# Row normalization on one core: the first store goes to ScalarE's queue, and VectorE alone does the last scale of its tile

## The chip, the cores and the metric

The kernel runs on one core of a Trainium2 chip. The metric is device time in microseconds (us), the median of several executions. A run counts as slow when it is over 1.5% above the fastest run of the same kernel; all runs quoted are fast unless the text says otherwise. A queue, here, is the line of transfers that one engine (SP or ScalarE) has issued; the 16 DMA engines carry out the transfers of all queues, one packet after another. A ratio is the mean time of one kernel's fast runs over the mean of the other's fast runs in the same rounds, so it is not quite the ratio of the medians quoted beside it.

## The reference

Each row of a 1024 x 4096 float32 matrix is divided by its length:

```python
norm = np.sqrt(np.sum(x ** 2, axis=-1, keepdims=True) + eps)
return (x / norm).astype(np.float32)
```

So 16.78 MB are read and 16.78 MB are written.

## The kernel before

There are two tiles ("tile 0" and "tile 1"), each with four rows per partition: 128 x (4 x 4096) float32, 8.39 MB. Both loads are issued at once on the queue of the SP engine. For each tile VectorE squares row 3 and ScalarE squares rows 0, 1 and 2, each with a running sum; ScalarE takes the roots, VectorE the reciprocals, and VectorE scales the rows in place. Only the last row to be ready in tile 0, row 2, is scaled by both engines:

```python
def scale_by_both(self, r):
    cut = 7 * self.D // 8
    rstd = self.rstd[:, r : r + 1]
    self.nc.scalar.activation(out=self.x[:, r, :cut], in_=self.x[:, r, :cut],
                              func=ACT_F.Copy, scale=rstd)
    self.nc.vector.tensor_scalar_mul(out=self.x[:, r, cut:],
                                     in0=self.x[:, r, cut:], scalar1=rstd)
...
for i in range(n_tiles):
    g = RowGroups(nc, io, stats, scratch, D, R, eps_t)
    load = nc.sync.dma_start(out=g.flat(), in_=x_t[i])
    ...
for i, g in enumerate(groups):
    ...
    g.square_act(2)
    g.norm(2)
    if i < n_tiles - 1:
        g.scale_by_both(2)
    else:
        g.scale(2)
    store = nc.sync.dma_start(out=out_t[i], in_=g.flat())
```

Four transfers of 8.39 MB stand in one queue: load 0, load 1, store 0, store 1. Each is spread over 16 DMA engines, and each engine moves 8 packets of 64 KiB per transfer, then one tiny packet that writes the semaphore.

## Time and profile before

| | before |
|---|---|
| time, median | 81.8 us (81.79 to 81.83) |
| span of the profiled execution | 80.2 us |
| DMA engines in packets, mean of 16 | 97.4% of the span, 78.1 us |
| VectorE / ScalarE busy | 33% / 37% |
| store 0 issued / load 1 seen landed | 38.99 / 41.40 us |

The queue line of the page says how long packets were under way, as a share of 16 engines' span. Multiplied by the span it is the packet time per engine.

### The profile page before, as it was taken

The page shows a single profiled execution, that of the slowest core. Times are in us where ns is not written, and L with a number is a line of the kernel's source. Part 1 is how long each engine was busy: PE and PEld are TensorE (multiplying, and loading weights), DVE is VectorE, ACT ScalarE, POOL GpSimd, SP SyncE. Part 2 cuts the span into 40 slices and gives each one's busy share as a digit, 9 for nine tenths or more (in the row PEclk, how much of TensorE's full clock was granted, in tenths as well). Part 3 has the DMA queues.
Part 4 walks back from the last instruction along what each step waited for, and adds up shares of the span by engine and source line. Part 5 has one row for each costly group of instructions (what it writes and reads, how often), then busy time and mean ns, then how long its engine had stood idle before and what let it go on. Part 6 is the DMA issues. An engine that isn't in the chain of part 4 may idle for free.

```text
span 80.2 us, 93 instructions
## 1 busy us (share of the span) xinstructions
DVE 26.7 (33%) x21; ACT 29.7 (37%) x23; POOL 0.2 (0%) x4
## 2 busy tenths in 40 slices
DVE  0000000000099599960039995999200000000000
ACT  6000000000099999989439999950000000000000
POOL 0000000000000000000000000000000000000000
DMA  9099996699996699996699990999991999992990
GB/s 490 33 523 523 523 490 294 261 523 523 523 490 261 294 523 523 523 490 261 294 523 523 523 490 33 523 523 523 523 458 65 523 523 523 523 425 98 523 523 0
DMA packets 576, 33.55 MB, mean 418 GB/s; under 512 B 64, under 2 KB 64, under 8 KB 64
## 3 DMA queue, kind: packets, MB, share of 16 engines
q1 hardware_dynamic: 576, 33.55, 97.4%
HBM read 16.78 MB, written 16.78 MB: 418 GB/s over the span
## 4 chain that ended last, share of the span: by engine, by line
DMA 51%; ACT 10%; DVE 9%; issue 0%
DMA xt<-in_x_dram 51%; ACT sq_act L33 9%; DVE xt L64 9%; ACT rstd L53 1%; DVE rstd L59 0%
## 5 line engine op out<-in xcount | busy, mean ns | idle before, releaser
L33 ACT ACTIVATE sq_act<-xt 128x4096 f32<-128x4096 f32 x6 | 21.7, 3609 | 22.4 <-DMA xt<-in_x_dram 22.4
L42 DVE SCALAR_TENSOR_TENSOR sq_dve<-xt 128x4096 f32<-128x4096 f32 x2 | 8.9, 4426 | 26.4 <-DMA xt<-in_x_dram 26.4
L64 DVE TENSOR_SCALAR xt<-xt,rstd 128x4096 f32<-128x4096 f32 x7 | 16.5, 2353 | 0.2
L72 ACT ACTIVATE xt<-xt,rstd 128x3584 f32<-128x3584 f32 x1 | 3.3, 3283 | 0.2 <-DVE rstd L59 0.2
L53 ACT ACTIVATE rstd<-ssq,eps_t 128x1 f32<-128x1 f32 x8 | 2.1, 290 | 0.1
L59 DVE RECIPROCAL rstd<-rstd 128x1 f32<-128x1 f32 x8 | 1.3, 160 | 2.5 <-ACT rstd L53 2.5
L33 ACT ACT_TABLE_LOAD x1 | 1.3, 1283 | 0.8 <-PEq L258 0.8
L53 ACT ACT_TABLE_LOAD x1 | 1.3, 1283 | 0.0
L33 ACT ACTIVATION_READ_ACCUMULATOR sq_act<-xt 128x1 f32 x6 | 1.1, 187 | 0.0
L78 DVE TENSOR_SCALAR xt<-xt,rstd 128x512 f32<-128x512 f32 x1 | 0.5, 487 | 0.0
L211 DVE MEMSET eps_t<- 128x1 f32 x1 | 0.1, 59 | 0.9 <-PEq L258 0.9
L42 DVE DVE_READ_ACCUMULATOR sq_dve<-xt 128x1 f32 x2 | 0.2, 83 | 0.0
L258 POOL MEMSET const-uint8-127<- 128x1 uint8 x1 | 0.1, 103 | 0.0
L258 POOL MEMSET const-bfloat16-1.0<- 128x1 bf16 x1 | 0.1, 102 | 0.0
L258 POOL MEMSET const-float32-0.0<- 128x1 f32 x1 | 0.1, 99 | 0.2 <-issue 0.2
L258 POOL MEMSET const-float32-1.0<- 128x1 f32 x1 | 0.1, 99 | 0.0
## 6 DMA issues: line engine op xcount, KB each, us to landing
xt<-in_x_dram SPq DMA_DIRECT2D x2, 31.3
out_dram<-xt SPq DMA_DIRECT2D x2, 22.5
```

The source lines that it names most:

```text
L33: self.nc.scalar.activation(out=sq_a, in_=self.x[:, r], func=ACT_F.Square, accum_out=self.ssq[:, r : r + 1],)
L42: self.nc.vector.scalar_tensor_tensor(out=sq_v, in0=self.x[:, r], scalar=1.0, in1=self.x[:, r], op0=ALU.mult, op1=ALU.mult, accum_out=self ...
L53: self.nc.scalar.activation(out=self.rstd[:, r : r + n], in_=self.ssq[:, r : r + n], func=ACT_F.Sqrt, bias=self.eps_t,)
L59: self.nc.vector.reciprocal(out=self.rstd[:, r : r + n], in_=self.rstd[:, r : r + n])
L64: self.nc.vector.tensor_scalar_mul(out=self.x[:, r], in0=self.x[:, r], scalar1=self.rstd[:, r : r + 1])
L72: self.nc.scalar.activation(out=self.x[:, r, :cut], in_=self.x[:, r, :cut], func=ACT_F.Copy, scale=rstd,)
L78: self.nc.vector.tensor_scalar_mul(out=self.x[:, r, cut:], in0=self.x[:, r, cut:], scalar1=rstd)
L211: nc.vector.memset(eps_t, eps)
L258: nc = _bacc.Bacc("TRN2", target_bir_lowering=False, num_devices=1)
```

## The change

The intent is to have tile 0 ready sooner (VectorE needs 2.35 us for the row; the shared scale needs 3.28 us on ScalarE) and to let its store go out without standing behind load 1 in SP's queue. The helper `scale_by_both` goes away, and:

```diff
-        if i < n_tiles - 1:
-            g.scale_by_both(2)
-        else:
-            g.scale(2)
-        store = nc.sync.dma_start(out=out_t[i], in_=g.flat())
+        g.scale(2)
+        queue = nc.scalar if i < n_tiles - 1 else nc.sync
+        store = queue.dma_start(out=out_t[i], in_=g.flat())
```

More of the change, by code (lines that the diff above doesn't have):

```diff
@@ L65, in scale @@
             out=self.x[:, r], in0=self.x[:, r], scalar1=self.rstd[:, r : r + 1]
-        )
-    def scale_by_both(self, r):
-        cut = 7 * self.D // 8
-        rstd = self.rstd[:, r : r + 1]
-        self.nc.scalar.activation(
-            out=self.x[:, r, :cut],
-            in_=self.x[:, r, :cut],
-            func=ACT_F.Copy,
-            scale=rstd,
-        )
-        self.nc.vector.tensor_scalar_mul(
-            out=self.x[:, r, cut:], in0=self.x[:, r, cut:], scalar1=rstd
         )
```

## The prediction

> **What bounds the kernel now.** I read the page's slices and its queue line first, because a kernel that loads and stores every byte once is likely to be held by its transfers.
>
> ```profile
> DMA  9099996699996699996699990999991999992990
> ...
> q1 hardware_dynamic: 576, 33.55, 97.4%
> ```
>
> One digit is 2.0 us. Digits drop to 6, 0 or 1 now and then, but a packet here is 64 KiB and long, and is booked unevenly; the second line is the safe one: on the mean of 16 engines the packets took 97.4% of the span, 0.974 x 80.2 = 78.1 us of 80.2. The 576 packets are 512 of 64 KiB (33.55 MB / 65,536) and 64 tiny ones, which are the semaphore writes: 16 for each of 4 transfers (2 loads, 2 stores, 8.39 MB each). So each engine moves 8 data packets per transfer, 32 in all, and one packet takes 78.1 / 32 = 2.44 us. Read one by one, the packet records say 2.418 us for nearly all of them, so a transfer lasts 8 x 2.418 = 19.3 us and four last 77.4 us.
>
> Then the groups of instructions, for the engines:
>
> ```profile
> DVE 26.7 (33%) x21; ACT 29.7 (37%) x23; POOL 0.2 (0%) x4
> ...
> L33 ACT ACTIVATE sq_act<-xt 128x4096 f32<-128x4096 f32 x6 | 21.7, 3609 | 22.4 <-DMA xt<-in_x_dram 22.4
> L42 DVE SCALAR_TENSOR_TENSOR sq_dve<-xt 128x4096 f32<-128x4096 f32 x2 | 8.9, 4426 | 26.4 <-DMA xt<-in_x_dram 26.4
> L64 DVE TENSOR_SCALAR xt<-xt,rstd 128x4096 f32<-128x4096 f32 x7 | 16.5, 2353 | 0.2
> L72 ACT ACTIVATE xt<-xt,rstd 128x3584 f32<-128x3584 f32 x1 | 3.3, 3283 | 0.2 <-DVE rstd L59 0.2
> ```
>
> Both engines are idle for two thirds of the time and wait for loads. Last the timeline around the first store:
>
> ```profile
> 35.68 3.28 ACT L72 ACTIVATE xt<-xt,rstd 128x3584 f32<-128x3584 f32 x1 [0.23 <-DVE rstd L59]
> ...
> 38.99 0.35 SPq L240 DMA_DIRECT2D out_dram<-xt  x1
> 41.40 3.62 ACT L33 ACTIVATE sq_act<-xt 128x4096 f32<-128x4096 f32 x1 [2.43 <-DMA xt<-in_x_dram]
> ...
> 54.38 2.35 DVE L64 TENSOR_SCALAR xt<-xt,rstd 128x4096 f32<-128x4096 f32 x1
> 56.76 0.34 SPq L240 DMA_DIRECT2D out_dram<-xt  x1
> ```
>
> The reader is to see three things. The first store is issued at 38.99, but load 1 has landed only at 41.37 (the squares start at 41.40), and both sit on the one SP queue, so the store is behind the load: it is 2.4 us early. In the packet records the load's last data packets end at 40.26 to 41.05 and the store's first start at 40.48 to 41.06: no hole worth having. The second store is issued at 56.76, while the first store's last packets end at 59.80 to 60.36: it has 3.0 to 3.6 us of slack. So the queue is never empty from about 1 to 79.7 us, and the end is set by 32 packets in a row on each engine. The chain of waits walks back through tile 1's arithmetic, but that is not what binds: the last store waits for the queue, not for its data.
>
> **What the Trainium skill says.** (1) "DMA: Bandwidth & Descriptors", section Specifications: a fabric ceiling of 435 GB/s. The trace agrees: 65,536 B x 16 / 2.418 us = 434 GB/s. There is no bandwidth left to win. (2) Same page, Issuing engines are not separate DMA queues: transfers from SP and ACT run on the same 16 engines and interleave; a second queue saves only issue time. The trace has only one queue, so it can't show this; it shows issues of 0.34 us, off the path. (3) Same page, Queues, rings and completion order: each DMA engine goes round-robin between its rings, one packet at a time, and the semaphore increment is a last small descriptor of the transfer's own ring. No run so far shows two rings, but the 64 tiny packets are these descriptors; this is where my main risk comes from. (4) "VectorE: DVE Perf Modes", The perf-mode tier table: a float32 tensor_scalar in SBUF runs at 2x (1227 ns for 2048 elements). The trace agrees: 2353 ns for 4096 is far under one element per 0.96 GHz cycle (4267 ns).
>
> **The change, part by part.** *Scale of tile 0, row 2.* Removed: ACT 3283 ns beside DVE 487 ns, both starting at 35.68. Added: one DVE scale of the L64 kind, 2353 ns, from the same 35.68, after the same reciprocal; DVE is idle there until 41.40, so it delays nothing. The tile is ready at 35.68 + 2.35 = 38.03 rather than 38.97, 0.93 us earlier. ACT is freed, which is worth nothing: its next work waits for load 1.
>
> *Queue of store 0.* It is issued by ACT at about 38.05 to 38.1, with 0.35 us of issue time, done before ACT's next square at 41.4 or later. The new thing is that the store no longer stands behind load 1. How soon do its packets reach the engines? The first load, issued at 0.00 on empty engines, had its first packets start at 1.0 to 2.1 us. That gives 39.1 to 40.2 for the store (an estimate). Load 1's eighth and last data packet started at 37.85 to 38.62 on every engine, so all its data are already moving and end at 40.26 to 41.05 as before. What is not yet done is its semaphore write. If each engine takes turns, then after the last data packet it takes a store packet (2.42 us) and only then the load's semaphore write. Load 1 would be reported landed at 41.37 + 2.42 = 43.79.
>
> *Tile 1.* From the squares to the issue of its store it takes 56.76 - 41.40 = 15.36 us, all of it arithmetic that the change leaves alone. A load that lands 2.42 us late gives store 1 an issue at 59.18. The engines, always busy in between, finish store 0 at the same 59.80 to 60.36. With 1.0 to 2.1 us from issue to first packet, store 1 starts at 60.2 to 61.3 instead of 59.8 to 60.4: a hole of 0.4 to 0.9 us, straight on the end. If the start-up is shorter than at the kernel's beginning[...], the hole closes. So the sum for this way: total data 77.4 us unchanged, -0 for the earlier store, +0 to +0.9: 81.8 to 82.7 us.
>
> **The rivals.** *A, no delay of the load.* The engines may have lined up the semaphore write right after the last data packet before the store's descriptors arrive. For it: the write follows its data within tens of ns in the records before. Then load 1 lands at 41.4, store 1 is issued at 56.8, the two stores share the engines for their last microseconds, and as these stay busy the end is the same: 81.8 (at best 81.6, if the 0.2 us hole of the earliest engines counted, which it should not since the latest engine had none). I give it about a third.
>
> *B, one packet of delay,* or part of one if two rings share an engine at finer grain: as worked out, 81.8 to 82.7. About half.
>
> *C, more delay.* If two store packets go ahead of the semaphore write, load 1 lands at 46.2, store 1 is issued at 61.6 and starts at 62.6 to 63.7: +2.8 to +3.3 us, about 85. If an engine drained all 8 store packets before going back, load 1 would land near 60.7 and the end would be near 97. Against: a record is 64 KiB, so a turn of one packet is already long, and nothing speaks for turns of eight. Together about 12%.
>
> *D, a gain.* The tile is ready earlier, and a hopeful reading is that the end moves by that 0.93 us. Against it: the store already waited 2.4 us for the queue. With data packets filling 77.4 of the 80.2 us, the rest is start-up (1 to 2 us), the landing of the last store and the ending; the change touches none of these. About 2%.
>
> **Range and chances.** A puts 81.8 at a third; B puts 81.8 to 82.7 at a half, middle 82.3; C a tail at 85 and above. The median of these is 82.2. The range from 81.6 to 83.2 leaves the tail of C outside and little below. 2% faster is 80.2 us, which would need a whole 1.6 us of the empty time; I give it 0.02. 2% slower is 83.4, which needs C, or B with a start-up of about 3 us: 0.12. The rest, 0.86, is within 2%.
>
> **What would show it.** In the changed profile: two queues in the queue list, of about 25.2 and 8.4 MB; the row-2 scale of tile 0 as an eighth L64 instruction, with the ACT and DVE pieces of L72 and L78 gone; store 0 issued on ACT's queue near 38.1. The step that decides is the start of tile 1's squares: 41.4 says A, about 43.8 says B, 46 or more says C. Then the issue of store 1, 15.36 us after that start. If it comes before about 58.5 the engines should show no hole near 60 us; at 59.2 a small one. The mean packet should stay near 2.42 us; if packets of the two queues overlap and stretch instead, the turns are finer than a packet. I would be wrong if the packets became faster or slower with two queues, since everything rests on 77.4 us of unchanged data time, or if the engines left holes when they change between rings.

## The result and the profile after

| | before | after |
|---|---|---|
| time, median of 5 | 81.83 us | 82.76 us |
| ratio (95%) | | 1.0116 (1.0101 to 1.0131) |
| span | 80.2 us | 80.9 us |
| store 0 issued | 38.99 us | 37.75 us |
| load 1 seen landed (tile 1's squares start) | 41.40 us | 41.54 us |
| store 1 issued | 56.76 us | 56.96 us |

The changed kernel is 0.93 us slower: clear of the noise, though within 2%. (The two spans differ by 0.7 only, because the profiled execution of before was a long one, 82.04 us: its slowest DMA engine began its last load packet at 38.62, that of the changed kernel at 38.33.) From the page after, the span, the slices and the queues:

```profile
span 80.9 us, 91 instructions
...
DMA  9099999299999299999099909999909999909990
...
q1 hardware_dynamic: 432, 25.17, 72.9%
q10 hardware_dynamic: 144, 8.39, 24.8%
```

The second queue, q10, is ScalarE's and carries store 0. The two shares add up to 97.7% of 80.9, or 79.0 us of packet time per engine, against 78.1 before. The bytes are the same. So the 0.9 us did not go into a hole: the packets themselves took longer. The timeline after, around the first store and at the issue of the second (start, duration, engine, line, operation):

```profile
35.37 2.35 DVE L64 TENSOR_SCALAR xt<-xt,rstd 128x4096 f32<-128x4096 f32 x1
37.75 0.37 ACTq L224 DMA_DIRECT2D out_dram<-xt  x1
41.54 3.62 ACT L33 ACTIVATE sq_act<-xt 128x4096 f32<-128x4096 f32 x1 [6.41 <-DMA xt<-in_x_dram]
...
54.58 2.35 DVE L64 TENSOR_SCALAR xt<-xt,rstd 128x4096 f32<-128x4096 f32 x1
56.96 0.35 SPq L224 DMA_DIRECT2D out_dram<-xt  x1
```

Store 0 goes out 1.24 us earlier (0.93 of it from the scale; the rest because load 0 landed 0.3 us sooner in this execution, which differs from run to run). Tile 1 starts at nearly the same time and takes 15.42 us to its store, before 15.36. The scheduler put the small square roots of tile 1 in another order, so that ScalarE waits 0.8 us for VectorE there, but it costs nothing: store 1 is issued 3.8 us before the engines have finished store 0.

The packet records, read one by one, show where the time went. The handover is the place where a DMA engine turns from one transfer to the next. In this and all later tables, "loss at the handover" is worked out as the start of an engine's second store packet, minus the start of its seventh load-1 packet, minus three packets of 2.4185 us; mean of 16 engines.

```
                                before          after
last packet of load 1, mean     2.43 us         2.76 us (2.60 to 3.00)
first packet of store 0, mean   2.43 us         3.11 us (2.83 to 3.31)
all packets around them         2.42 us         2.42 us
loss at the handover            0.08 us         1.03 us
load 1's semaphore writes       40.26 to 41.05  40.62 to 41.23, right after the data
store 0's last data end         59.79 to 60.37  60.77 to 60.97
store 1's first packets start   59.79 to 60.37  60.77 to 60.97, no hole
```

The mean loss grew by 0.95 us and the time by 0.93. The whole result is two packets per engine, at the handover from loading to storing. The two figures need not agree this well: the time follows the engine that ends last, and the loss is a mean of 16 (in the scale-only run below, the mean loss grew by 0.37 and the time by 0.56; there the last engine began its last load packet at 38.38, and the last such packet ended at 41.41, which is 0.61 more than one packet of 2.42).

### The profile page after: what moved, and what is told of

Its sections match the earlier page's. It is cut to its first block, busy times and chain, and to the rows that moved or that the text cites. A ratio compares the mean times of both kernels' runs of the same rounds, so it can differ in the third digit from the quotient of the medians.

```text
span 80.9 us, 91 instructions
## 1 busy us (share of the span) xinstructions
DVE 28.7 (35%) x21; ACT 26.5 (33%) x22; POOL 0.2 (0%) x4
## 3 DMA queue, kind: packets, MB, share of 16 engines
q1 hardware_dynamic: 432, 25.17, 72.9%
q10 hardware_dynamic: 144, 8.39, 24.8%
## 4 chain that ended last, share of the span: by engine, by line
DMA 50%; ACT 10%; DVE 9%; issue 0%
DMA xt<-in_x_dram 50%; ACT sq_act L33 9%; DVE sq_dve L42 5%; DVE xt L64 3%; ACT rstd L53 1%; DVE rstd L59 0%
## 5 line engine op out<-in xcount | busy, mean ns | idle before, releaser
L64 DVE TENSOR_SCALAR xt<-xt,rstd 128x4096 f32<-128x4096 f32 x8 | 18.8, 2353 | 0.3
```

The costliest lines, as they stand in the source:

```text
L64: self.nc.vector.tensor_scalar_mul(out=self.x[:, r], in0=self.x[:, r], scalar1=self.rstd[:, r : r + 1])
```

## The experiments

The candidates after the result were: a queue that starts slowly when first used (the kernel's very first packets take 3.07 us on the mean too); load and store packets at work together; the earlier issue by itself; the second queue by itself. Each experiment is described by its edit to the kernel before or to the changed one.

### One half alone: the queue

To the kernel before:

```diff
-        store = nc.sync.dma_start(out=out_t[i], in_=g.flat())
+        queue = nc.scalar if i < n_tiles - 1 else nc.sync
+        store = queue.dma_start(out=out_t[i], in_=g.flat())
```

> Store 0 goes to ScalarE's queue, but tile 0's row 2 is still scaled by both engines, so it is issued at about 39.0 us instead of 37.75. After the change, load 1's last data packets took 2.76 us on the mean and store 0's first ones 3.11 (before: 2.43 and 2.43): 1.0 us lost per engine, and nothing else in the trace moved. Cold-queue theory (the first packet of a queue never used before starts slowly, as the kernel's very first packets do: 3.07 us): the loss is still there, about 0.7 to 1.0 us, first store packets near 3.1 us; time 82.6 to 82.9. Mixing theory (load and store packets of two queues at work on the same engine slow each other): the store arrives 1.25 us later, so it overlaps the load by at most half as long, load packets near 2.45 to 2.6, loss 0.3 to 0.6; time 82.1 to 82.5.

Measured: 82.57 us against 81.86, ratio 1.0086 (1.0074 to 1.0098). The queue lines of its page and the issue in its timeline:

```profile
q1 hardware_dynamic: 432, 25.17, 72.7%
q10 hardware_dynamic: 144, 8.39, 25.0%
...
38.69 0.37 ACTq L241 DMA_DIRECT2D out_dram<-xt  x1
```

97.7% of its span of 80.7 us is 78.8 us of packets. The last load packets took 2.42 us, the first store packets 3.24; loss 0.82. So the second queue alone costs 0.7 us, with the store issued at 38.69, nearly as late as before. By the expectation this spoke for the slow first use of a queue (loss 0.7 to 1.0) and against mixing (0.3 to 0.6); the used queue and the swapped queues below decided otherwise. Nor is it one fixed start-up time from the issue: in the changed kernel the store was issued 0.94 us earlier than here, yet its first packets ended later (43.88 to 44.07, here 43.59 to 43.89).

### One half alone: the scale

To the changed kernel:

```diff
-        queue = nc.scalar if i < n_tiles - 1 else nc.sync
+        queue = nc.sync
```

> The other half alone: VectorE scales row 2 of tile 0 alone, both stores stay on the SP queue. Store 0 is then issued at about 37.8 to 38.1 us and waits behind load 1 in the same queue. Every theory that puts the loss on the second queue expects the time of the kernel before, 81.8 within 0.15, load and store packets at the handover near 2.43 us. If the loss came from the earlier issue by itself (descriptors made while load 1 still runs), this one would be near 82.7.

Measured: 82.42 us, ratio 1.0064 (1.0052 to 1.0076). This was a surprise: with one queue only, the earlier tile still costs 0.56 us. Page and timeline:

```profile
q1 hardware_dynamic: 576, 33.55, 97.5%
...
37.82 19.60 SPq L224 DMA_DIRECT2D out_dram<-xt  x2
41.73 4.43 DVE L42 SCALAR_TENSOR_TENSOR sq_dve<-xt 128x4096 f32<-128x4096 f32 x1 [3.94 <-DMA xt<-in_x_dram]
```

Store 0 is issued at 37.82, when load 1's last packets are just about to start (37.80 to 38.38). Those packets took 2.88 us instead of 2.43; the store's own took 2.42; loss 0.45. Load 1 is seen at 41.73 rather than 41.40.

### A queue that has been used before

To the changed kernel:

```diff
+            warm = scratch_pool.tile([P, 128], F32)
+            nc.scalar.dma_start(out=warm, in_=x_t[0][:, :128])
```

> The changed kernel with one small load (512 bytes per partition, 64 KiB in all, into a tile nobody reads) issued on ScalarE's queue at the start, so that the queue has been used before store 0. Its own cost should be 0.1 to 0.4 us of engine time. Cold-queue theory: the loss of 1.0 us at the handover is gone, packets there near 2.43 us; time 81.9 to 82.2. Mixing theory: the handover is as in the changed kernel, 2.76 and 3.11 us; time 82.8 to 83.2.

Measured: 82.91 us, ratio 1.0126 (1.0113 to 1.0139). Last load packets 2.58, first store packets 3.23, loss 0.96. The small load itself cost 0.07 us, where load 0 gives way to load 1. The slow first use of a queue is out. The same trace shows, at the later handover, where the order of a semaphore write and the next transfer changes:

```profile
57.19 0.35 SPq L226 DMA_DIRECT2D out_dram<-xt  x1
```

Store 1, on the other queue, was issued 1.26 to 1.58 us before the engines began store 0's last packets (58.45 to 58.77). On 15 engines store 0's semaphore write came one packet of store 1 after its data, on one directly after it.

### The queues swapped

To the changed kernel:

```diff
-        queue = nc.scalar if i < n_tiles - 1 else nc.sync
+        queue = nc.sync if i < n_tiles - 1 else nc.scalar
```

> Store 0 on SP, store 1 on ScalarE's queue, which nothing used before; scales as in the changed kernel. The change of queue now lies between two stores, near 60 us, and store 1 is issued about 3 us before store 0 ends. Cold-queue theory: store 1's first packets take about 3.1 us and the loss of 0.7 to 1.0 us appears there; time 82.5 to 82.9. Mixing theory (load against store): no loss, packets 2.42 to 2.45 at both handovers; time 81.7 to 81.9.

Measured: 82.34 us, ratio 1.0064 (1.0047 to 1.0081). The change of queue between the two stores cost nothing: 2.42 us for all packets there, on a queue never used before. I had expected no loss at all under the mixing account; but the 0.49 us at the other handover is that of the scale-only run, since the store is again issued early (37.77). So a change of queue from store to store, issued some 3 us ahead, is free.

```profile
57.05 0.37 ACTq L224 DMA_DIRECT2D out_dram<-xt  x1
```

Store 0's last packets began at 57.58 to 58.27, 0.53 to 1.22 us after this issue, and all 16 of its semaphore writes followed the data directly.

### The scale alone, its store held back

To the scale-only kernel, after tile 0's last scale:

```diff
+        if i < n_tiles - 1:
+            part = g.x[:, 2, :1536]
+            nc.vector.tensor_scalar_mul(out=part, in0=part, scalar1=1.0)
```

> The scale-only kernel (both stores on SP, VectorE alone scales row 2; 82.42) with a pass of VectorE over 1536 columns times 1.0 after that scale, which holds store 0 back by about 1.0 us to 38.8 us, near the 38.99 of before. If the early issue alone made the scale-only kernel slow, the last load packets go back to 2.43 us and the time to 81.8 within 0.15. If VectorE's longer use of the tile or anything else in the scale did it, it stays near 82.4.

Measured: 81.86 us, ratio 0.9994 (0.9976 to 1.0011). Its timeline:

```profile
38.98 18.06 SPq L227 DMA_DIRECT2D out_dram<-xt  x2
41.34 4.43 DVE L42 SCALAR_TENSOR_TENSOR sq_dve<-xt 128x4096 f32<-128x4096 f32 x1 [2.39 <-DMA xt<-in_x_dram]
```

Useless work on VectorE that delays the store by 1.16 us wins back the whole 0.56 us: loss 0.07, as before. The cause in the scale's half is the moment of issue and not the scale.

### Load behind load, with the same timing

To the kernel before, so that load 1 arrives late in load 0:

```diff
-        load = nc.sync.dma_start(out=g.flat(), in_=x_t[i])
+        if i == 1:
+            for _ in range(4):
+                nc.vector.memset(sq_dve, 0.0)
+            nc.vector.tensor_copy(out=g.x[:, 0, :600], in_=sq_dve[:, :600])
+        queue = nc.sync if i == 0 else nc.sync
+        load = queue.dma_start(out=g.flat(), in_=x_t[i])
```

> The kernel before, with load 1 held back by idle work of VectorE (four memsets and a small copy into its tile) until about 18.4 us, that is, until load 0's last data packets start; all on the SP queue. So one load arrives behind another with the same lead as store 0 has behind load 1 in the scale-only kernel (issued 37.82, last load packets stretched to 2.88 us). If the stretch comes from a transfer arriving that early, whatever its direction: load 0's last packets near 2.8 us, time about 82.3. If it needs a store arriving during a load (mixing of directions): those packets stay at 2.42 to 2.45, time 81.8 within 0.2.

Measured: 81.91 us, ratio 1.0009 (0.9993 to 1.0026). Load 1 was issued at 18.93, somewhat later than aimed at (load 0's last packets start at 18.45 to 19.18), so it doesn't quite match the scale-only run's lead. Those packets took 2.43, the next 2.42: no loss. The kernel before brackets it from the other side: there load 1 is issued 20 us ahead and load 0's last packets also take 2.42. Neither timing of a load behind a load showed the stretch; the lead of the scale-only run itself, wholly before the last packets, was not tried with two loads on one queue.

The same with the two loads on different queues (load 0 on ScalarE's queue, not moved to the front, hence about 0.7 us later; load 1 on SP, held back in the same way with copies of 1800, 4000 and 1250 columns):

```diff
-        load = nc.sync.dma_start(out=g.flat(), in_=x_t[i])
-        if i == 0:
-            first_load_to_front(nc, load.ins)
+        queue = nc.scalar if i == 0 else nc.sync
+        load = queue.dma_start(out=g.flat(), in_=x_t[i])
```

> Load 0 on ScalarE's queue (not moved to the front, so everything starts some 0.8 us later), load 1 on SP held back to about 19.0 us, when load 0's last data packets start. A change of queue between two loads with the timing that store 0 has in the changed kernel (stretch 2.76 on the old queue's last packets, 3.11 on the new one's first). If a change of queue with a late arrival costs 0.7 us whatever the direction, load 1's first packets are near 3.1 us. If it needs load against store, 2.42 to 2.5. The time of before plus 0.8 for the late start, plus what this shows.

Measured: 82.80 us, ratio 1.0112 (1.0098 to 1.0126), most of it the later start. Load 0's last packets 2.42, load 1's first 2.67: a loss of 0.25 us. That is neither answer quite: a change of queue costs something between two loads too, but about a third of what it costs from load to store.

> As the run before it, with load 1 issued about 1.1 us later, at 20.2, some 0.5 to 1.0 us after load 0's last data packets started: the timing of store 0 in the queue-only kernel, whose first store packets took 3.24 us while the last load packets stayed at 2.42. Late arrival on another queue as the cause: first packets of load 1 near 3.2 us. Direction as the cause: near 2.42 to 2.5.

Measured: 83.81 us, ratio 1.0248 (1.0208 to 1.0289). This run failed as a test. Load 1 was issued at 20.63 and its first packets started at 21.73 to 22.53, for some engines well after load 0's data had ended (21.71 to 22.05); the 2.91 us of those packets mixes this lateness with the handover. It gave one more point by accident: its store 0, on SP behind load 1 on SP, was issued at 39.31 with load 1's last packets starting at 39.02 to 39.78, and those took 2.76 us.

> As the two runs with load 0 on ScalarE's queue and load 1 on SP, with load 1 issued 2.5 to 3.0 us before load 0's last packets end, the very lead that store 0 has in the changed kernel (there 2.76 us on the old queue's last packets and 3.11 on the new one's first). At a lead of 2.2 to 2.7 us load 1's first packets took 2.67. Direction account: 2.42 and 2.42 to 2.67, a loss of at most 0.25 us; time about 82.5 to 82.8. Late-arrival account, whatever the direction: about 2.76 and 3.1; time about 83.5.

Measured: 83.00 us, ratio 1.0134 (1.0118 to 1.0150). Load 1 issued at 19.20, load 0's last packets ending 21.55 to 22.29: 2.42 and 2.67, a loss of 0.26. The issue in its timeline:

```profile
19.20 0.37 SPq L224 DMA_DIRECT2D xt<-in_x_dram  x1
```

At about the lead of the changed kernel, load after load on another queue loses 0.26 us, store after load 1.03. (Here the second queue is SP's and the first ScalarE's, the other way round; for two loads only this way was tried.)

### The store issued much earlier

To the changed kernel (a wrong result: row 2 of tile 0 is stored as loaded), once as it stands and once with both stores on SP:

```diff
-        g.square_act(2)
-        g.norm(2)
-        g.scale(2)
+        if i == n_tiles - 1:
+            g.square_act(2)
+            g.norm(2)
+            g.scale(2)
```

> The same early store (row 2 left unscaled, a wrong result on purpose) on the SP queue, behind load 1, issued at about 34.9 us. In the scale-only kernel, issued at 37.82, the last load packets took 2.88 us and the first store packets 2.42. If that loss is one fixed price for a store whose packets are known before the last load packet has begun, it is the same here: last load packets near 2.88, nothing else long, time 82.3 to 82.5. If it grows with the time that the store waits behind the load, the packet before the last is long too, and the time is above 82.8. If it only came from the store being issued at that very moment, everything is at 2.42 and the time 81.8.

Measured, on SP: 83.13 us, ratio 1.0150 (1.0135 to 1.0165). Its page and timeline:

```profile
span 81.3 us, 87 instructions
...
q1 hardware_dynamic: 576, 33.55, 97.5%
...
34.67 23.51 SPq L225 DMA_DIRECT2D out_dram<-xt  x2
42.48 4.43 DVE L42 SCALAR_TENSOR_TENSOR sq_dve<-xt 128x4096 f32<-128x4096 f32 x1 [7.84 <-DMA xt<-in_x_dram]
```

One queue, the store 3 us earlier than in the scale-only run, and the last load packets took 3.55 us. The packet at work when the store was issued took 2.43, the next one 2.42, and the store's first 2.42, so the issue as such, 3 us before the long packet, stretched nothing by more than 0.01 us. Loss 1.12. None of the three answers fitted: the price is neither fixed nor does it spread over more packets; it grows, on the one last packet.

> The changed kernel without the square, norm and scale of tile 0's row 2 (a wrong result on purpose: that row is stored as it was loaded), so that store 0 is issued on ScalarE's queue at about 34.9 us, some 5.3 to 6 us before load 1 would end, instead of 2.5 to 3.0. So far the handover to the other queue cost 0.69 to 0.82 us on the first store packets when issued 1.6 to 3 us before the load's end. Late-arrival account: with so long a lead the first store packets are back at 2.42 and only the mixing on load packets (0.3 to 0.5 us per engine) is left. Direction account: each load or store packet at work beside one of the other queue's and other direction stretches, so two to four packets per engine are long and the loss per engine is 1 us or more. In both, store packets take turns with load 1's last ones, load 1 lands at 43 to 46.5 us, store 1 is issued after 58.5, and a hole of up to 2.5 us near 60 us may follow; time 82.5 to 85.

Measured, on ScalarE's queue: 85.2 us as the median of runs from 83.38 to 85.63; the profiled run counts as slow by its time, so its time is compared with nothing, and only the order and length of its packets are used. Its timeline:

```profile
34.75 0.37 ACTq L225 DMA_DIRECT2D out_dram<-xt  x1
47.42 4.42 DVE L42 SCALAR_TENSOR_TENSOR sq_dve<-xt 128x4096 f32<-128x4096 f32 x1 [12.70 <-DMA xt<-in_x_dram]
62.84 0.35 SPq L225 DMA_DIRECT2D out_dram<-xt  x1
```

Here the mechanism of the prediction's rival B is seen. On 15 engines a whole store packet went between load 1's last data (ended 41.42 to 41.88) and its semaphore write (43.83 to 44.29); on one engine the write came at 47.04. That engine put a store packet before load 1's last packet already, at 39.10, and there it was the load packet in front of it, the seventh, that took long (3.23 us). So at this lead it was the load packet in front of the first store packet that stretched, whichever number it had. Load 1 was seen at 47.42, store 1 issued at 62.84, and its packets started at 63.68 to 63.83 while store 0's data had ended at 60.74 to 61.53: a hole of over 2 us. The mean loss at the first handover was 1.11, no more than on one queue with the same lead.

### All handovers side by side

Issue and packets of the handover from load 1 to store 0. The fourth column is the issue, less the starts of load 1's last packets (first and last of 16 engines); negative is earlier.

```
kernel             store 0   issued   less start of      last load  first store  loss
                   on                 last load packet   packet     packet
before             SP        38.99    +1.15 .. +0.37     2.43       2.43         0.08
scale, held back   SP        38.98    +1.16 .. +0.43     2.42       2.43         0.07
late load, same    SP        38.87    +1.09 .. +0.36     2.43       2.42         0.04
late load, lead    SP        39.55    +0.87 .. -0.09     2.42       2.42         0.00
late load, other   SP        39.46    +0.63 .. +0.11     2.42       2.42         0.00
(accident)         SP        39.31    +0.29 .. -0.47     2.76       2.42         0.34
scale only         SP        37.82    +0.02 .. -0.56     2.88       2.42         0.45
queues swapped     SP        37.77    +0.01 .. -0.56     2.92       2.42         0.49
much earlier       SP        34.67    -3.05 .. -3.70     3.55       2.42         1.12
queue only         ScalarE   38.69    +0.85 .. +0.34     2.42       3.24         0.82
used queue         ScalarE   38.13    +0.26 .. -0.59     2.58       3.23         0.96
after              ScalarE   37.75    -0.06 .. -0.58     2.76       3.11         1.03
```

(The three lines "late load" are the stores of the runs with load 1 issued at 18.93 on the same queue, and at 19.20 and 19.49 on another. The much earlier store on ScalarE's queue is left out, since one of its engines changed the order of the packets.) On one queue, the loss is nil as long as the store is issued after the last load packets have started (the 0.04 to 0.08 of the latest issues is a short hole on the engines that finished first), is 0.3 to 0.5 us when the issue falls about on their start, and 1.1 us when it is 3 us earlier. On the other queue it is 0.8 us even with an issue nearly as late as before's, and 1.0 when earlier. That some engines store while others still load costs nothing by itself: in the line with the issue at 39.55, the loads ended and the stores began at 41.12 to 42.07, engine by engine, and all these packets took 2.42.

## Why the prediction was right or wrong

**What held.** Before is bound by its transfers, with packets of 2.42 us in a row, and the earlier tile could gain nothing. The scale ran as an eighth row of 2.35 us and store 0 was issued 0.93 us sooner relative to tile 0's arithmetic; two queues of 25.17 and 8.39 MB appeared; tile 1's arithmetic took 15.4 us. The time, 82.76, lies in the range, but by luck: the upper part of the range was there for a late load and a hole before store 1, and neither came. The forecast was 82.2, a growth of 0.4 us where 0.93 was measured, and the way it was reached was wrong. The prediction did name the sign that came true ("if the packets became faster or slower with two queues", or "overlap and stretch"), but gave it no cost and no chance.

**The step that was expected to cost and did not.** "Load 1 would be reported landed at 41.37 + 2.42 = 43.79": it was at 41.5. Its semaphore writes followed the data directly, as rival A had it, and with that the hole of "0.4 to 0.9 us" before store 1 fell away. The turns between queues exist: in the changed kernel store 0's own semaphore writes (63.18 to 63.38) come one packet of store 1 after its data, store 1 having been issued 3.8 us before these data ended; the much earlier store shows it at load 1. In all handovers between two queues here, the order goes with how far the issue lies ahead of the start of the last data packet. With 1.40 us or more the write always came a packet later (changed kernel 1.40 to 1.59, queue only 1.53 to 1.82); with 1.22 or less never (swapped 0.53 to 1.22); in the used-queue run, with 1.26 to 1.58, on 15 engines of 16 (the exception had 1.35). Store 0 of the changed kernel was issued 0.06 to 0.58 us ahead, and load 1's write went first. The prediction had asked only whether its packets would arrive before the data ended.

**The step that failed.** "The engines, always busy in between, finish store 0 at the same 59.80 to 60.36", resting on "total data 77.4 us unchanged". The data packets took 78.09 us per engine before (the first ones are long) and 79.03 after. Store 0 ended at 60.77 to 60.97, because two packets per engine together took 1.03 us longer than two others. I had taken 2.42 us for every packet at the handover, since the trace of before shows 2.43 there; but that trace shows a single timing, and a lucky one. The prediction's only worry was the second queue, and there chiefly the order of the semaphore write. An earlier issue on the same queue it held to be free ("-0 for the earlier store"); the scale-only run shows 0.56 us. (Two small slips bear on nothing: the "end near 97" of rival C is a time in the span, about 99 in device time. And that a transfer's semaphore write is each engine's last descriptor stands in the skill page's section "Why a DMA increments its semaphore by 16 and not by 1", not in the one on queues.)

**What took its place.** Both parts of the change set it off. Alone, the earlier issue costs 0.56 us (gone when the issue is held back to 38.98) and the queue 0.71. Together they make 0.93, less than their sum, 1.27: the mean loss did not pass 1.12 in any handover from load to store that was tried. In these runs the large loss came only with a store behind a load: a store behind a store lost nothing on one queue or two; a load behind a load nothing on one queue (at two leads) and 0.26 us on two. It is not a first-use cost, not a hole, and not more bytes.

**What stays open.** Why a load packet and a store packet that are both known to an engine take up to 1.1 us more than one after the other was not seen: the records give one start and one duration per packet, not what reads and writes do inside it. That they overlap and get in each other's way is the account that fits all lines of the table, but it is argued, not shown. Nor was a direct test made of a store on ScalarE's queue issued later than 38.69; since its engines would soon run empty, there seems to be little to win. No run beat the kernel before: the held-back one equals it, with 0.07 us of loss left at this handover.

## What to carry to other kernels

This kernel keeps its DMA engines full; making a store ready sooner, or giving it a queue of its own, gained nothing and cost 0.56 and 0.71 us. In a kernel like it, look at the length of the packets where the transfers turn from loading to storing, and compare the queues' share times the span before and after, since a loss there leaves no hole to be seen. Here the handover lost least (0.00 us) when the first store was issued just after the last load's final packets had started, behind the load in its own queue. Before trusting a quiet spot of a trace in a prediction, ask whether the change moves its timing; a cheap delay in the kernel can test it.

## What the Trainium skill lacked or had wrong

- "DMA: Bandwidth & Descriptors", section Issuing engines are not separate DMA queues, tells that transfers from several queues interleave on the same engines and that a second queue saves only issue time. It doesn't say that the turn from loading to storing can cost: per engine 0.00 to 0.08 us with a late issue on one queue, 0.34 to 0.49 with the issue about at the start of the last load packet, 1.12 when 3 us earlier, and 0.82 to 1.03 through a second queue.
- The same page, section Queues, rings and completion order, has the engines go round-robin between queues by packet. The runs agree when the other transfer was issued 1.40 us or more before the last data packet began (a semaphore write came one packet, 2.42 us, after its data); with 1.22 us or less the write went first, and with 1.26 to 1.58 on one engine of 16. The page doesn't say how far ahead an engine settles its order.
- The same page, section Specifications, gives about 0.6 us from issue to first byte for SP and ScalarE. From an issue on free engines to the first packets the runs show 0.84 to 0.99 us (the store after the hole in the much earlier run) and 1.01 to 2.12 us at the start of the kernel before.
- No page read for this case tells that the very first packets of a kernel can be long: 3.07 us on the mean here instead of 2.42. It is not so for all packets on free engines: those of the store after the hole took 2.45.
